# Table swish, a new stage order, ordered first loads and bf16 weight copies spread over four uses, in a two-layer three-branch encoder step

## The chip, the cores and the metric

One Trainium2 chip, with all 8 of its cores on the same program, each with its own two prompt sequences and its own rows of the sample request. Cores 0 to 3 are one die and cores 4 to 7 the other. The time is the device time in microseconds (us) of the slowest core.

In some executions the four cores of one die (or of both) show a lower granted TensorE clock and the time is some per cent longer. A run is called slow when one die is over 1% longer than the other at a lower clock, or when it is over 1.5% above the fastest run of the same kernel. Only fast runs are compared.

## The reference, cut to what matters

```python
# per layer, D = 1024; [..] cut
h = rmsnorm(x)
proj = h @ w_in            # split into the 12 column groups used below
# A: gated short convolution, 3 taps
y_a = a_b * dwconv3(a_c * a_x) * silu(a_z)
# B: Conformer convolution module, 31 taps
glu = b_in[..., :W] * sigmoid(b_in[..., W:])
y_b = silu(layernorm(dwconv31(glu) + bias, ln_b_g, ln_b_b)) * silu(b_z)
# C: chunked spatial gating, 128-token chunks
y_c = gelu(c_u) * (w_s @ layernorm(gelu(c_v)) + b_s) * silu(c_z)
m = sum_k sigmoid(g_k + gate_b_k) * (y_k @ w_branch_k)
x = x + m @ w_out
```

Each core has 9 token tiles: 5 of 512 tokens, 3 of 384 and one of 448 (384 of a prompt and the 64 sample rows). The weights arrive as float32.

## The kernel before

The kernel goes through 18 "bodies", one for each tile and layer, all on one PE stream without a break. I number them b0 to b17. The order is tile 0 and tile 1 with layer 0 (b0, b1), the same tiles with layer 1 (b2, b3), tiles 2 and 3 with layer 0 (b4, b5), with layer 1 (b6, b7), and so on. The 512-token bodies are b0 to b8 and b10. The 384-token bodies are b9 and b11 to b15, and the 448-token bodies are b16 and b17.

A body's stages are CV (projection of v), then B1 (GLU input of branch B, four steps q) interleaved with A (branch A, eight steps j), conv_b (31-tap convolution of B, eight steps, as matmuls), C, the gate Z of branch B, merge gates G with branch projections BR, and O.

All weights pass through a ring of four slots. The first use of a weight block loads it as float32 and casts to bf16 on the way, on the queue that GpSimd (POOL) issues. A bf16 copy is stored from the slot at once, on the queue that SyncE (SP) issues. Every later use reloads that copy through SP.

```python
def emit_load(n):
    l, key = plan[n]
    s = n % NSLOT                                    # NSLOT = 4
    dst_bf, w = wloc(l, key, True)
    if (l, key) not in converted:                    # first use
        converted.add((l, key))
        src, w = wloc(l, key, False)
        DMA(wring[:, s, 0:w], src, (), (("w", s),), "w%d" % s, eng="pool")
        DMA(dst_bf, wring[:, s, 0:w], (("w", s),), (("wall", l, key),), "ws%d" % s)   # store, on SP
    else:
        DMA(wring[:, s, 0:w], dst_bf, (("wall", l, key),), (("w", s),), "w%d" % s)    # reload, on SP
```

The convolution of B reads four shifted copies of the GLU output. A group of 16 DMAs per step q, all issued by SP one after another, makes them. I call one such group a replica (grep<-gluT in the profile). Times to land, below, are those of one of its 16 DMAs, of 67.6 KB.

```python
def replicate(q):
    qb = q % 2
    # [..]
    for s4 in range(4):
        for g in range(GB):                          # GB = 4
            # grep[32*s4 : 32*s4+32, :, g] <- gluT[32*g : 32*g+32, qb, :, s4 : ]
    S.dma_group("sp", fns, (("gluT", qb),), ("grep",), "rep%d" % qb)

stage_B1(0)
replicate(0)
stage_A(0)
stage_A(1)
# [..]
for q in range(1, 4):
    stage_B1(q)
    conv_b(2 * q - 2)                                # waits for replicate(q - 1)
    conv_b(2 * q - 1)
    replicate(q)
    for j in (2 * q, 2 * q + 1):
        stage_A(j)
        # [..]
conv_b(6)
conv_b(7)
```

The swish functions are made from tanh on ScalarE (ACT) and a scalar_tensor_tensor (STT) on VectorE (DVE). The layer norm of B takes a DVE reciprocal.

```python
# stage A:
ACT(z, bank_ap(bz, NT), AF.Tanh, PSR(bz), RT(tz), scale=0.5)
STT(z, z, 1.0, bank_ap(bz, NT), ALU.add, ALU.mult, ...)
# layer norm of B, after stage C 0:
ACT(var, var, AF.Sqrt, ...)
RECIP(rstd_bc[:, 0:NT], var, ...)
# per chunk j, during stage C:
TT(c, c, mean_bc, ALU.subtract, ...); STT(c, c, ln_g[j], rstd_bc, ALU.mult, ALU.mult, ...); TS(c, c, ln_b[j], ALU.add, ...)
# gate of B (stage Z), per chunk:
ACT(c, co[:, j], AF.Tanh, scale=0.5); ACT(z, bank_ap(bz, NT), AF.Tanh, scale=0.5)
STT(z, z, 1.0, bank, ...); STT(c, c, 1.0, co[:, j], ...); STT(yb[:, j], c, 0.25, z, ...)
```

Of the kernel before, what the change touches and what calls it, by code (L numbers as in the profile page):

```python
# [6 lines left out]
F32 = mybir.dt.float32  # L7
BF16 = mybir.dt.bfloat16
AF = mybir.ActivationFunctionType
ALU = mybir.AluOpType  # L10
# [21 lines left out]
class Sched:  # L32
    ENG = ("pe", "act", "dve", "pool", "sp")

    def __init__(self):
        self.streams = {e: [] for e in self.ENG}
        self.count = {e: 0 for e in self.ENG}
        self.known = {e: {} for e in self.ENG}
        self.last_w = {}
        self.readers = {}  # L40
        self.lane_n = {}
        self.bank_ptr = 0
        self.held = set()
        self.tmp_ptr = 0

# [88 lines left out]
    def tmp(self):  # L134
        i = self.tmp_ptr
        self.tmp_ptr = (i + 1) % NTMP
        return i
# [10 lines left out]
def build_program(n_seq, seq_len, with_sample=True, samp_len=64):  # L148
# [38 lines left out]
    with es:  # L187
# [129 lines left out]
        for l, T in bodies:  # L317
            plan += [(l, ("CV", 0)), (l, ("CV", 1))]
            for q in range(4):
                plan += [(l, ("B1", q)), (l, ("A", 2 * q)), (l, ("A", 2 * q + 1))]  # L320
            plan += [(l, ("CUZ", q)) for q in range(4)] + [(l, ("B2", 0)), (l, ("B2", 1))]
            for j in range(8):
                plan += [(l, ("G", j)), (l, ("BR", j))]
            plan += [(l, ("O", 0)), (l, ("O", 1))]
        converted = set()
        ring = dict(next=0, use=0)
        live = set()

        def emit_load(n):
# [3 lines left out]
            if (l, key) not in converted:  # L333
                converted.add((l, key))
                src, w = wloc(l, key, False)
                DMA(wring[:, s, 0:w], src, (), (("w", s),), "w%d" % s, eng="pool")
                DMA(dst_bf, wring[:, s, 0:w], (("w", s),), (("wall", l, key),), "ws%d" % s)
            else:
                DMA(wring[:, s, 0:w], dst_bf, (("wall", l, key),), (("w", s),), "w%d" % s)

        def ring_pump():
            while (ring["next"] < len(plan) and ring["next"] < ring["use"] + NSLOT
# [4 lines left out]
        def wget(l, key):  # L347
# [9 lines left out]
            w = 384 if key[0] in B384 else 512  # L357
            return wring[:, s, 0:8 * w].rearrange("p (k n) -> p k n", k=8), (("w", s),)
# [17 lines left out]
        def load_x(T, engs=("pool",)):  # L376
            for s, (c0, rows, xsrc, ydst) in enumerate(T["chunks"]):
                DMA(X[0:rows, T["xb"], s, :], xsrc, (), (("X", T["xb"], s),), "x%d" % s, eng=engs[s % len(engs)])

        load_x(tiles[0], ("sp", "act"))  # L380
        DMA(pc[:, :, :], prm.rearrange("p (c r) -> p c r", c=NCH), (), ("pc",), "p0", eng="act")
        ring_pump()
# [9 lines left out]
        DMA(cbq[:, :, :], cvb_in.rearrange("l p n -> p l n"), (), ("cbq",), "p1", eng="act")  # L392
        cow = co[:, :, :].rearrange("p c n -> p (c n)")
        for l in range(DEPTH):
            DMA(cow[:, l * 1024:(l + 1) * 1024], w_sq[l], (), (("co", 2 * l), ("co", 2 * l + 1)), "p%d" % (2 + l), eng="act")
            DMA(cow[:, 2048 + l * 1024:3072 + l * 1024], b_s[l].partition_broadcast(128), (),
                (("co", 4 + 2 * l), ("co", 5 + 2 * l)), "p%d" % (4 + l), eng="act")
        na, nb = DEPTH * NCH * (KA - 1), DEPTH * NCH * (KB - 1)
        DMA(tmp_t[:, 1, 0:na], ca_in, (), RT(1), "p6", eng="act")
        DMA(tmp_t[:, 2, 0:nb], cb_in, (), RT(2), "p7", eng="act")  # L400
        DMA(fg[:, :], final_g.partition_broadcast(128), (), ("fg",), "p8", eng="act")
        for l in range(DEPTH):
            r0 = l * NROW
            TS(pc[:, :, r0 + R_GB0:r0 + R_CA + KA], pc[:, :, r0 + R_GB0:r0 + R_CA + KA], 0.5, ALU.mult, ("pc",), ("pc",))
        S.tmp_ptr = 3

        def prep_caches():
            COPY(chal_a[:, :, :, :].rearrange("p a b c -> p (a b c)"), tmp_t[:, 1, 0:na], RT(1), ("chal",))
            TS(chal_b[:, :, :, :].rearrange("p a b c -> p (a b c)"), tmp_t[:, 2, 0:nb], 2.0, ALU.mult, RT(2), ("chal",))

        def prep_ws():
            for l in range(DEPTH):
                wl = cow[:, l * 1024:(l + 1) * 1024]
                rl = (("co", 2 * l), ("co", 2 * l + 1))
                S.op("pool", lambda e, wl=wl: e.affine_select(
                    out=wl.rearrange("p (g q) -> p g q", g=8), in_=wl.rearrange("p (g q) -> p g q", g=8),
                    pattern=[[0, 8], [1, 128]], compare_op=ALU.is_ge, fill=0.0, base=0, channel_multiplier=-1),
                    reads=rl, writes=rl)
                COPY(wsT[:, l].rearrange("p g q -> p (g q)"), wl, rl, (("wsT", l),))
                b2 = S.bank_n(2)  # L420

                def f(e, l=l, b2=b2):
                    ins = None
                    for h in range(2):
                        ins = e.matmul(bank_ap(b2 + h, 512), lhsT=ones[:, :],
                                       rhs=wsT[:, l, 4 * h:4 * h + 4, :].rearrange("p g q -> p (g q)"), start=True, stop=True)
                    return ins
                PE(f, (("wsT", l), "ones"), PSR(b2, b2 + 1))
                for j in range(8):
                    STT(Bc[:, l, j, :], ps[:, b2 * 512 + j * 128:b2 * 512 + (j + 1) * 128], pcol(l, j, R_LCB),  # L430
# [586 lines left out]
```

## Time and profile before

| | before |
|---|---|
| median of 3 runs | 4914.83 us (4901.43 to 5396.57) |
| profiled run, slowest core (core 1) | 4923.7 us |
| first matmul of CV; of branch B | 40 us; 71 us |
| b0, b2 (first use of a layer's weights) | 375, 364 us |
| b1, b3 to b8, b10 | 274 to 276 us |
| the six 384-token bodies | 218 to 227 us, 1337 in all |
| b16, b17 | 281, 327 us |

The durations of bodies here and below are differences between the starts of the first CV matmul of one body and of the next, read from the timeline of PE (TensorE).

From the page of the kernel before come the busy times and the chain of waits that ended last, followed back from the end and shared out by engine:

```profile
...
PE 4407.0 (90%) x25860; PEld 2134.8 (43%) x25860; DVE 2400.2 (49%) x4071; ACT 1636.5 (33%) x2684; POOL 167.2 (3%) x579
...
PE 69%; DVE 12%; DMA 6%; issue 6%; SPq 3%; ACT 3%; ACTq 1%; DVEq 0%; POOL 0%; POOLq 0%
...
```

PE is busy for 90% of the span and is 69% of the chain, so it is what bounds the kernel. The remaining 10% is what a change can win, together with PE's slow phases. What PE waited for is in the list of PE's waits of the kernel before (line waited for, then us in total, times, longest us):

```profile
...
PE ps L673 <- DMA grep<-gluT: 110.7, 13, 30.8
PE ps L484 <- DVE tmp_t L244: 109.8, 71, 3.5
PE ps L484 <- DVE yb L244: 80.9, 18, 5.5
...
```

The table of stretches splits this. Here it is for b2, b3 and for one stretch of b4 (busy us by engine with instruction counts, then granted clock, DMA share, GB/s):

```profile
...
core 1: us, PE busy (x) PEld busy (x) DVE busy (x) ACT busy (x) POOL busy (x), PEclk, DMA share, GB/s
...
689.00:1053.00 364.00, 274.72 (x1426) 120.36 (x1425) 146.91 (x219) 96.62 (x152) 23.50 (x60) 0.89 0.93 209
1053.00:1327.00 274.00, 260.40 (x1425) 117.03 (x1424) 143.14 (x216) 100.58 (x157) 8.50 (x32) 0.99 0.52 170
1448.00:1510.00 62.00, 50.47 (x245) 22.74 (x243) 54.77 (x82) 23.34 (x39) 0.00 (x0) 0.96 0.29 98
...
```

b2 does the same work as b3 and takes 90 us longer, with the DMA engines 93% busy: its weights come as float32 and are stored. That is one kind of loss. Of the 90 us, 56 are PE's waits for replicas, of which b3 has none. The last stretch is the other: from the middle of branch C to the first merge DVE is busy 54.77 of 62 us while PE is busy only 50.47. The timeline of PE of the kernel before shows what happens there (start, duration, operation, count, and in brackets the wait just before with its releaser):

```profile
...
1468.19 3.61 PE L484 MATMUL ps<-hT,wring 128*128 128x512 bf16 x16 [1.05 <-DVE tmp_t L244]
...
1473.36 3.61 PE L484 MATMUL ps<-hT,wring 128*128 128x512 bf16 x16 [1.33 <-DVE tmp_t L244]
...
1478.38 13.97 PE L484 MATMUL ps<-hT,wring 128*128 128x512 bf16 x64 [1.19 <-DVE tmp_t L244]
1495.20 6.74 PE L484 MATMUL ps<-hT,wring 128*128 128x512 bf16 x24 [2.84 <-DVE tmp_t L244]
1501.78 1.89 PE L484 MATMUL ps<-ya,wring 128*128 128x512 bf16 x8
...
1510.46 3.57 PE L484 MATMUL ps<-yb,wring 128*128 128x512 bf16 x8 [5.07 <-DVE yb L244]
...
```

Five times here PE waits for DVE, 11.5 us in all. After the last wait, of 5.07 us, eight matmuls take 3.57 us; the eight before took 1.89. After the wait of 2.84 us, 24 matmuls take 6.74 us. The granted clock (the share of full speed that TensorE was given) is 0.50 in the trace from 1495.2 to 1498 us and 0.99 in the 4 us after, and it is 0.50 again from 1510.4 to 1513.9. So a long wait costs twice: the wait, and a restart at half rate. The Trainium skill, "TensorE: Matmul & The Clock Gate", Part 1, states that an idle stretch of about 3.4 us drops the array to half rate until it has been busy that long again. This trace agrees in kind, since the 1.33 us wait above is followed by 16 matmuls at the usual pace (3.61 us), but here a wait of 2.84 us was already enough (roughly, since the profile models the ends of matmuls).

Here are the replicas in the same kernel. The first fence is from the list of DMA issues on the page (count, size, median us from issue to landing), and shows them beside the float32 loads:

```profile
...
wring<-w POOLq DMA_DIRECT2D x44, 1024.0 KB, 14.1
...
grep<-gluT SPq DMA_DIRECT2D x640, 67.6 KB, 2.4
...
```

The timeline of SP (b3 of the kernel before) has the issue of the first replica of the body, all 16 DMAs in a row:

```profile
...
1078.73 10.02 SPq L640 DMA_DIRECT2D grep<-gluT  x16
...
```

and the timeline of PE has the matmuls that have to cover it, with no wait in brackets ahead of the convolution (line 673):

```profile
...
1074.79 20.24 PE L484 MATMUL ps<-hT,wring 128*128 128x512 bf16 x93
1094.95 3.64 PE L673 MATMUL ps<-grep,dB_t 128*32 128x512 bf16 x64
...
```

Issuing takes SP 10 us. The last DMAs of the replica then have to land, and the convolution can start. Its cover is the stages A 0, A 1 and B1 1, each four projections of 8 matmuls: 96 matmuls of 216 ns, or 20.7 us. That was enough. The last replica of a body has a shorter cover in this kernel, two A stages only (64 matmuls); in the 384-token bodies, where these take 10.4 us, the convolution 6 behind them waits sometimes (8.74 us in b12, 7.73 in b15).

### The profile page before, as it was taken

The numbers are of one execution on the slowest core, as the hardware profiler recorded it, in microseconds if no ns is written. First come the engines' busy times: TensorE is split into PE (matmuls) and PEld (weight loads), VectorE is DVE, ScalarE is ACT, GpSimd is POOL, SyncE is SP. The second block draws the span as 40 slices with busy tenths as digits, with TensorE's granted clock in tenths as the row PEclk, the third lists the DMA queues.
The fourth block names the chain that finished last, engine by engine and source line by source line (L and its number), as shares of the span: only waits on it lengthen the run. The fifth ranks groups of instructions, "written<-read, shape, count | busy, mean of one in ns | idle before, by whom it ended". The sixth has DMA issues, their size and how long they took to land.

```text
span 4923.7 us, 75738 instructions; the slowest of 8 cores (4869.0 to 4923.7 us)
## 1 busy us (share of the span) xinstructions
PE 4407.0 (90%) x25860; PEld 2134.8 (43%) x25860; DVE 2400.2 (49%) x4071; ACT 1636.5 (33%) x2684; POOL 167.2 (3%) x579
## 2 busy tenths in 40 slices
PE   4789895889999999999999999989898989999898
PEld 1334342334444444443444554455455555544343
DVE  2353632536355464646354545444545454555362
ACT  2232331333332333333332333333333333332331
POOL 1000000000000000000000000000000000000000
PEclk8899997999999999999999999999999999998787
DMA  9897379985463535355464554365655647563443
GB/s 220 203 202 218 128 186 218 189 222 179 154 199 131 192 120 188 122 176 168 161 194 141 195 178 166 130 229 180 202 192 170 214 167 242 160 216 120 148 137 103
DMA packets 234727, 869.45 MB, mean 177 GB/s; under 512 B 34512, under 2 KB 108848, under 8 KB 178032
## 3 DMA queue, kind: packets, MB, share of 16 engines
q1 hardware_dynamic: 211680, 753.61, 46.1%
q0 software_dynamic: 20384, 104.61, 11.1%
q10 hardware_dynamic: 2288, 6.39, 0.5%
q8 instruction: 216, 3.54, 0.3%
q14 instruction: 159, 1.30, 0.1%
HBM read 768.97 MB, written 93.85 MB: 175 GB/s over the span
## 4 chain that ended last, share of the span: by engine, by line
PE 69%; DVE 12%; DMA 6%; issue 6%; SPq 3%; ACT 3%; ACTq 1%; DVEq 0%; POOL 0%; POOLq 0%
PE ps L484 54%; DVE tmp_t L244 6%; PE ps L834 5%; PE ps L673 5%; PE ps L534 4%; SPq L640 3%; DMA wring<-w 3%; DMA grep<-gluT 2%; DMA c<-wring 1%; DVE co L244 1%; DVE co L241 1%; DVE yc L241 1%; PE ps L658 1%; ACT cs_t L238 1%; ACTq L264 1%
## 5 line engine op out<-in xcount | busy, mean ns | idle before, releaser
L484 PE MATMUL ps<-hT,wring 128*128 128x512 bf16 (+2 forms) x13824 | 2851.8, 366 | 149.3 <-DVE tmp_t L244 109.8
L484 PEld LDWEIGHTS ps<-hT,wring 128*128 128x128 bf16 x13824 | 1364.9, 100 | 1560.3 <-issue 248.2
L244 DVE SCALAR_TENSOR_TENSOR tmp_t<-tmp_t,ps 128x512 f32<-128x512 f32 (+2 forms) x864 | 544.4, 632 | 1291.9 <-PE ps L484 646.8
L238 ACT ACTIVATE tmp_t<-ps 128x512 f32<-128x512 f32 (+2 forms) x882 | 475.0, 554 | 1096.6 <-PE ps L484 941.5
L238 ACT ACTIVATE tmp_t<-ps,pc 128x512 f32<-128x512 f32 (+2 forms) x432 | 275.0, 645 | 850.3 <-PE ps L484 835.1
L673 PE MATMUL ps<-grep,dB_t 128*32 128x512 bf16 (+2 forms) x5120 | 265.3, 356 | 119.4 <-DMA grep<-gluT 110.7
L484 PE MATMUL ps<-yb,wring 128*128 128x512 bf16 (+2 forms) x1152 | 279.2, 391 | 80.9 <-DVE yb L244 80.9
L238 ACT ACT_TABLE_LOAD x161 | 206.6, 1283 | 243.0 <-PE ps L484 83.6
L534 PE MATMUL ps<-wring,hT 128*128 128x512 bf16 (+1 forms) x1056 | 242.0, 390 | 34.1 <-DVE hT L241 34.1
L834 PE MATMUL ps<-wring,vm 128*128 128x512 bf16 (+1 forms) x1056 | 243.9, 393 | 30.9 <-DVE vm L241 15.8
L484 PE MATMUL ps<-ya,wring 128*128 128x512 bf16 (+2 forms) x1152 | 255.8, 366 | 16.7 <-DMA wring<-w 12.0
L484 PE MATMUL ps<-yc,wring 128*128 128x512 bf16 (+2 forms) x1152 | 254.8, 365 | 0.0
L673 PEld LDWEIGHTS ps<-grep,dB_t 128*32 128x32 bf16 x5120 | 125.5, 100 | 253.8 <-issue 179.7
L244 DVE SCALAR_TENSOR_TENSOR tmp_t<-tT,pc,tmp_t 128x512 f32<-128x512 bf16 (+2 forms) x320 | 209.1, 654 | 34.9 <-DVE tmp_t L244 0.2
L238 ACT ACTIVATE co<-ps,pc 128x512 f32<-128x512 f32 (+2 forms) x144 | 93.1, 646 | 380.0 <-PE ps L673 380.0
L484 PEld LDWEIGHTS ps<-yb,wring 128*128 128x128 bf16 x1152 | 118.5, 104 | 215.4 <-issue 114.1
L241 DVE TENSOR_TENSOR tT<-ps,tmp_t 128x512 bf16<-128x512 f32 (+2 forms) x160 | 94.6, 591 | 213.5 <-PE ps L484 143.2
L238 ACT ACTIVATE tmp_t<-co 128x512 f32<-128x512 f32 (+2 forms) x144 | 84.7, 589 | 284.3 <-DVE yb L244 127.9
L534 PEld LDWEIGHTS ps<-wring,hT 128*128 128x128 bf16 (+1 forms) x1056 | 105.4, 100 | 165.3 <-issue 50.0
L834 PEld LDWEIGHTS ps<-wring,vm 128*128 128x128 bf16 (+1 forms) x1056 | 105.1, 101 | 164.4 <-issue 58.4
L484 PEld LDWEIGHTS ps<-ya,wring 128*128 128x128 bf16 x1152 | 113.7, 99 | 136.2 <-issue 23.8
L238 ACT ACTIVATE cs_t<-ps,pc 128x512 bf16<-128x512 f32 (+2 forms) x288 | 169.3, 644 | 0.0
(92 smaller groups left out, 2658.6 us busy)
## 6 DMA issues: line engine op xcount, KB each, us to landing
wring<-c SPq DMA_DIRECT2D x352, 1024.0 KB, 6.0
wring<-c SPq DMA_DIRECT2D x256, 768.0 KB, 4.3
wring<-w POOLq DMA_DIRECT2D x44, 1024.0 KB, 14.1
c<-wring SPq DMA_DIRECT2D x44, 1024.0 KB, 10.7
grep<-gluT SPq DMA_DIRECT2D x640, 67.6 KB, 2.4
dB_t<-dball SPq DMA_DIRECT2D x128, 256.0 KB, 7.4
wring<-w POOLq DMA_DIRECT2D x32, 768.0 KB, 13.2
c<-wring SPq DMA_DIRECT2D x32, 768.0 KB, 13.3
```

The source lines that it names most:

```text
L238: S.op("act", lambda e: e.activation(out=out, in_=in_, func=func, **kw), reads=reads, writes=writes)
L241: S.op(eng, lambda e: e.tensor_tensor(out=out, in0=in0, in1=in1, op=op), reads=reads, writes=writes)
L244: S.op("dve", lambda e: e.scalar_tensor_tensor(out=out, in0=in0, scalar=scalar, in1=in1, op0=op0, op1=op1), reads=reads, writes=writes)
L264: S.op(eng, lambda e: e.dma_start(out=out, in_=in_), reads=reads, writes=writes, lane=lane)
L484: ins = e.matmul(bank_ap(b, NT), lhsT=w[:, kk, col0:col0 + 128], rhs=rhs[:, kk, 0:NT], start=(kk == 0), stop=(kk == 7))
L534: ins = e.matmul(ps[0:rows, (b2 + h) * 512:(b2 + h + 1) * 512], lhsT=hT[:, kk, c0:c0 + rows], rhs=wV[h][0][:, kk, :], start=(kk == 0), sto ...
L640: return e.dma_start(out=grep[32 * s4:32 * s4 + 32, :, g, 0:wb], in_=gluT[32 * g:32 * g + 32, qb, :, s4:s4 + wb])
L658: e.matmul(bank_ap(bS1, NT), lhsT=ones[:, :], rhs=cs_t[:, 2 * ci, 0:NT], start=(j == 0), stop=(j == 7))
L673: ins = e.matmul(ps[32 * g:32 * g + 32, b * 512 + c0:b * 512 + c0 + n], lhsT=dB_t[:, d, (g * MB + m) * 32:(g * MB + m + 1) * 32], rhs=grep ...
L834: ins = e.matmul(ps[0:rows, (b2 + h) * 512:(b2 + h + 1) * 512], lhsT=mT[:, kk, c0:c0 + rows], rhs=wO[h][0][:, kk, :], start=(kk == 0), sto ...
```

## The change

The intent was to take work off DVE where PE waits for it, to spread the DMA work of the first two layers over more bodies, and to bring the first matmul forward:

1. Swish by the Silu table of ACT in A and in the gate of B. The scale and bias of B's layer norm go into that Silu. The reciprocal standard deviation is Exp(-0.5 Ln(var + eps)) on ACT.
2. Another stage order. A 1 moves behind the first convolutions, convolutions 6 and 7 move ahead of stage A 7 with the layer norm right behind it, and the first merge gates move into stage Z.
3. The first loads are put in a sequence instead of all at once.
4. The bf16 copies are stored at the first, second, third or fourth use of a block, issued when the block is used. Until its copy exists, each use of the block is a float32 load: 188 of them instead of 76. In bodies 0 to 3 the small halo copies (the last tokens of one tile, which the convolutions of the next need) move from POOL to ACT.

```diff
             plan += [(l, ("CV", 0)), (l, ("CV", 1))]
-            for q in range(4):
-                plan += [(l, ("B1", q)), (l, ("A", 2 * q)), (l, ("A", 2 * q + 1))]
+            plan += [(l, ("B1", 0)), (l, ("A", 0))]
+            for q in range(1, 4):
+                plan += [(l, ("B1", q)), (l, ("A", 2 * q - 1)), (l, ("A", 2 * q))]
+            plan += [(l, ("A", 7))]
[..]
+        def store_visit(key):
+            return (2, 0, 3, 1, 2, 1)[order.index(key) % 6]
 
         def emit_load(n):
[..]
-            if (l, key) not in converted:
-                converted.add((l, key))
-                src, w = wloc(l, key, False)
-                DMA(wring[:, s, 0:w], src, (), (("w", s),), "w%d" % s, eng="pool")
-                DMA(dst_bf, wring[:, s, 0:w], (("w", s),), (("wall", l, key),), "ws%d" % s)
-            else:
+            if (l, key) in stored:
                 DMA(wring[:, s, 0:w], dst_bf, (("wall", l, key),), (("w", s),), "w%d" % s)
+                return
+            src, w = wloc(l, key, False)
+            DMA(wring[:, s, 0:w], src, (), (("w", s),), "w%d" % s, eng="pool")
+            visits[l, key] = visits.get((l, key), 0) + 1
+            if visits[l, key] > store_visit(key):
+                stored.add((l, key))
+                to_store.add(n)
[..]  in wget, at the use of a block:
+            if n in to_store:
+                DMA(wloc(l, key, True)[0], wring[:, s, 0:8 * w], (("w", s),), (("wall", l, key),), "ws%d" % s)
[..]
+            def hcopy(out, in_, reads, writes):
+                if bi < 2 * DEPTH:
+                    ACT(out, in_, AF.Copy, reads, writes)
+                else:
+                    COPY(out, in_, reads, writes, eng="pool")
[..]  stage A:
-                ACT(z, bank_ap(bz, NT), AF.Tanh, PSR(bz), RT(tz), scale=0.5)
+                ACT(z, bank_ap(bz, NT), AF.Silu, PSR(bz), RT(tz))
-                STT(z, z, 1.0, bank_ap(bz, NT), ALU.add, ALU.mult, RT(tz) + PSR(bz), RT(tz))
[..]
             stage_A(0)
-            stage_A(1)
[..]
             for q in range(1, 4):
                 stage_B1(q)
                 conv_b(2 * q - 2)
                 conv_b(2 * q - 1)
                 replicate(q)
-                for j in (2 * q, 2 * q + 1):
+                for j in (2 * q - 1, 2 * q):
                     stage_A(j)
[..]
             conv_b(6)
             conv_b(7)
[..]  layer norm of B and stage C:
-            ACT(tmp_t[:, tv, 0:NT], tmp_t[:, tv, 0:NT], AF.Sqrt, RT(tv) + ("epsc",), RT(tv), bias=epsc[:, 0:1])
-            RECIP(rstd_bc[:, 0:NT], tmp_t[:, tv, 0:NT], RT(tv), ("rstd_bc",))
+                ACT(tmp_t[:, tv, 0:NT], tmp_t[:, tv, 0:NT], AF.Ln, RT(tv) + ("epsc",), RT(tv), bias=epsc[:, 0:1])
+                ACT(rstd_bc[:, 0:NT], tmp_t[:, tv, 0:NT], AF.Exp, RT(tv), ("rstd_bc",), scale=-0.5)
[..]
-                STT(c, c, pcol(l, j, R_LBG), rstd_bc[:, 0:NT], ALU.mult, ALU.mult, ...)
-                TS(c, c, pcol(l, j, R_LBB), ALU.add, ...)
+                TT(c, c, rstd_bc[:, 0:NT], ALU.mult, ...)
[..]
+            stage_A(7, stat_b)
+            ln_b()
+            co_norm(0)
+            co_norm(1)
+            tail_out()
+            for j in range(8):
                 if j % 2 == 0:
                     wC = wget(l, ("CUZ", j // 2))
                 stage_C(j, *wC)
-                co_norm(j - 1)
+                if j < 6:
+                    co_norm(j + 2)
[..]  stage Z:
-                ACT(c, co[:, j, 0:NT], AF.Tanh, (("co", j),), RT(tc), scale=0.5)
-                ACT(z, bank_ap(bz, NT), AF.Tanh, PSR(bz), RT(tz), scale=0.5)
-                STT(z, ...); STT(c, ...); STT(yb[:, j, 0:NT], c, 0.25, z, ...)
+                ACT(c, co[:, j, 0:NT], AF.Silu, ..., scale=pcol(l, j, R_LBG), bias=pcol(l, j, R_LBB))
+                ACT(z, bank_ap(bz, NT), AF.Silu, PSR(bz), RT(tz))
+                TT(yb[:, j, 0:NT], c, z, ALU.mult, ...)
```

## The prediction

> **What bounds it now.** TensorE. The chain of waits gives PE 69%, DVE 12%, DMA 6%; PE is busy 4407 of 4924 us. The kernel is 18 bodies (9 token tiles x 2 layers); I read five kinds of loss from busy time by stretch and PE's waits (core 1):
> - Head: the first matmul of the first projection starts at 40 us, of branch B at 71.
> - Bodies 0 and 2 (first use of a layer's weights: float32 load plus bf16 store of the same slot) take 344 us (from 71) and 363, with DMA 91-93% busy; the same work in bodies 1 and 3 takes 275. The longest waits there are for the replicas of gluT (110 us in all): their queue also carries the stores, which wait for loads.
> - The eight other 512-token bodies take 275 us. In branch C, B-gate and first merge (1448 to 1510 of body 4) DVE is continuously busy and PE waits for it six times, 12 us, and twice restarts at half rate. Matmuls at their spacing (216 ns) would need about 256 us.
> - The six 384-token bodies take 219 to 227; spacing alone (162 ns) says about 193.
> - The last two (448) take 277 and 332; cores 0 and 1 run at clock 0.81 from 4480 on. Cores 2 and 3 ran at 0.76 to 0.80 from 100 to 500 us. The Trainium skill, "TensorE: Matmul & The Clock Gate" (HAM part), states a 13/16 limit for the whole die; here it held a pair of cores for some 450 us.
>
> **What the change does, per 512 body.** DVE loses 8 STT in A (0.69 us), 16 in B-gate, the 3.35 us reciprocal, 8 TS (0.49): about 24 of 142 us, nearly all inside or just before the stretch where DVE limits. Branch C plus LN falls from 4.75 to about 4.2 us per chunk against PE's 3.67; B-gate from 2.06 to 0.69 against 1.73. Moving conv 6/7 ahead starts LN one stage earlier. Costs: Silu and tanh share a table, so about one more table load per body (1.28 us here; "ScalarE: Activation LUTs", What ACT_TABLE_LOAD costs, says 1283 ns, and the trace agrees), off the path. Expected: 275 to about 261; 384 bodies 222 to about 204.
>
> Weights: 188 float32 loads instead of 76, stores spread over four uses. From queue shares a float32 load costs about 5.5 to 6 us of all engines per 1 MB block, a bf16 load or a store 3. Bodies 0 to 3 then each need about 250 us of DMA: near the limit, so I expect about 275 to 280 each, not 261. Bodies 0, 2 gain about 70 and 85; 1 and 3 nothing. Head: ordered loads save about 28 us.
>
> Sum: head 28, bodies 0 and 2 155, six 512 bodies 80, six 384 bodies 108, last two 40, about 410 to 430.
>
> **Predicted: 4490 us**, 8 in 10 within 4390 to 4640. Faster by over 2%: 0.95; within 2%: 0.04; slower: 0.01.
>
> **What would show it.** Branch B starts near 43 us; bodies 0 and 2 near 275, DMA about 0.9 there and raised in 1 and 3; steady 512 bodies 258 to 264 and PE's waits for tmp_t and yb by DVE falling from 190 us to under 60; waits for the replicas under 50; DVE busy about 2000; table loads about 180; software queue about 210 MB.
>
> **What would make it wrong.** DMA saturating in bodies 0 to 3, so that second uses get slower than 275; GpSimd's in-order queue, which holds halo copies behind float32 loads in bodies 4 to 7; DVE waiting in order for Exp at the start of C, so that its backlog still stalls PE there; and the clock limit engaging longer because PE is denser: 450 us at 0.81 costs about 85.

## The result, and the profile after

| | before | after |
|---|---|---|
| fast runs | 4891.85, 4901.43, 4914.83 us | 4728.16, 4732.03 us |
| slow runs | 5396.57 us | 5070.09, 5121.56 us |
| ratio of fast runs | 1 | 0.9648 (95%: 0.9593 to 0.9703) |
| PE's waits for replicas | 110.7 us | 223.0 us |
| DVE busy | 2400.2 us | 2024.8 us |

A ratio here and below compares the fast runs of one kernel with the other's fast runs of the same rounds; it is within 0.0002 of the ratio of their means, and not quite that of the medians. The changed kernel is faster by 3.5%. The prediction, 4490 us, was 8.6% below the time before, and its range ended at 4640. The profiled run of after is a fast one, 4726.6 us on core 6, and all its cores have a mean granted clock of 0.968 to 0.972.

From the page of the kernel after come busy times, chain, and two lines of the list of DMA issues:

```profile
...
PE 4306.4 (91%) x25860; PEld 2117.0 (45%) x25860; DVE 2024.8 (43%) x3476; ACT 1708.8 (36%) x2816; POOL 214.1 (5%) x607
...
PE 65%; DMA 10%; SPq 7%; DVE 7%; issue 6%; ACT 4%; DVEq 0%; POOL 0%; ACTq 0%; POOLq 0%
...
wring<-w POOLq DMA_DIRECT2D x112, 1024.0 KB, 11.7
...
grep<-gluT SPq DMA_DIRECT2D x640, 67.6 KB, 3.9
...
```

DMA plus SP's sequencer is now 17% of the chain, against 9% before. PE's share of the chain fell, and DVE's nearly halved. One DMA of a replica takes 3.9 us to land in the median, against 2.4. PE's waits of the kernel after:

```profile
...
PE ps L715 <- DMA grep<-gluT: 223.0, 32, 21.4
PE ps L507 <- ACT tmp_t L241: 46.5, 55, 2.6
PE ps L507 <- DVE tmp_t L247: 19.9, 43, 1.2
...
```

The two losses that the change aimed at are small or gone. The waits for tmp_t by DVE fell from 109.8 to 19.9 us, with 46.5 us now waiting for tmp_t by ACT, and the 80.9 us for yb have left the list. But the waits for the replicas doubled, from 13 to 32 of them. The merge of b5 shows the first point. In the timeline of PE of the kernel after, this is the end of stage C and the first merge:

```profile
...
1672.85 3.61 PE L507 MATMUL ps<-hT,wring 128*128 128x512 bf16 x16 [0.31 <-DVE tmp_t L247]
...
1677.20 19.15 PE L507 MATMUL ps<-hT,wring 128*128 128x512 bf16 x88 [0.52 <-ACT tmp_t L241]
1696.19 1.89 PE L507 MATMUL ps<-ya,wring 128*128 128x512 bf16 x8
...
1699.64 1.89 PE L507 MATMUL ps<-yb,wring 128*128 128x512 bf16 x8
...
```

The waits here are half a microsecond and less, and the first projection of yb runs at full pace. The second point is in the table of stretches of the kernel after, for b1, b3 and b8 (the columns are those of before):

```profile
...
337.00:627.00 290.00, 262.04 (x1425) 118.14 (x1424) 119.01 (x188) 100.26 (x172) 20.62 (x37) 0.96 0.91 188
...
933.00:1229.00 296.00, 265.18 (x1426) 119.00 (x1425) 120.52 (x184) 107.62 (x183) 20.92 (x39) 0.95 0.87 192
2351.00:2615.00 264.00, 257.76 (x1417) 117.00 (x1416) 119.40 (x183) 98.18 (x150) 8.10 (x31) 1.00 0.54 175
...
```

b8 takes 264 us against 275.5 before. b1 and b3 take 290 and 296, where before they took 274. The DMA share there is 0.91 and 0.87, where it was 0.50 and 0.52, yet the bytes moved are only 188 and 192 GB/s, against 175 in b8 with a share of 0.54. The timeline of SP of the kernel after has two of the replicas of b1:

```profile
...
361.94 10.74 SPq L682 DMA_DIRECT2D grep<-gluT  x16
...
414.05 21.13 SPq L682 DMA_DIRECT2D grep<-gluT  x16
...
```

and the timeline of PE shows the convolution (line 715) waiting for the first of them:

```profile
...
354.67 16.57 PE L507 MATMUL ps<-hT,wring 128*128 128x512 bf16 x76
382.29 5.30 PE L715 MATMUL ps<-grep,dB_t 128*32 128x512 bf16 x64 [11.05 <-DMA grep<-gluT]
...
409.20 1.91 PE L715 MATMUL ps<-grep,dB_t 128*32 128x512 bf16 x32
...
```

The replica's issue took 10.74 us from 361.94, and only at 382.29 could the convolution start. DVE's last write of gluT ended 0.14 us before the issue, so SP was not held up by other work (in b2 of before it began 17 us after that write). Between them PE now has A 0 and B1 1 alone, 64 matmuls or 13.8 us, since A 1 moved behind the convolution. The 64 convolution matmuls after the wait took 5.30 us, and twice 1.91 in the next step. The third replica took SP 21.13 us to issue. The DMA view of the kernel after says what else was on the engines from 340 to 440 us (packets, MB, share of 16 engines; then the replicas' own landing time):

```profile
...
q0 software_dynamic: 1992, 11.47, 66.8%
q1 hardware_dynamic: 4279, 7.04, 27.8%
...
grep<-gluT SPq DMA_DIRECT2D x48, 67.6 KB, 10.0
...
```

The float32 loads (q0) take 66.8% of the engines' time, and a DMA of 67.6 KB needs 10.0 us to land. The 384-token bodies have no float32 loads at all, and still PE waits in b12, in the timeline of PE of the kernel after:

```profile
...
3349.09 4.14 PE L715 MATMUL ps<-grep,dB_t 128*32 128x384 bf16 x64 [5.42 <-DMA grep<-gluT]
...
3369.63 1.49 PE L715 MATMUL ps<-grep,dB_t 128*32 128x384 bf16 x32
...
3408.53 2.75 PE L715 MATMUL ps<-grep,dB_t 128*32 128x384 bf16 x32 [5.46 <-DMA grep<-gluT]
...
```

The first wait is at convolution 0, whose cover is 64 matmuls of 162 ns (10.4 us) instead of 96 (15.6 us), while SP's issue alone takes 10.19 us there. The second is at convolution 6. Its cover is 64 matmuls too (A 5 and A 6, line 507), as many as before (A 6 and A 7). Both restarts are slow: 64 convolution matmuls take 4.14 us after the first wait, and 32 take 2.75 after the second, where 32 take 1.49 without one.

Where the time went, by stretches. The column "predicted" has the terms of the prediction, with 277.5 for each of b0 to b3 (275 for b0) after a start of branch B at 43 us. The terms add up to 4509. The text took about the upper end of its savings, 4490.

| us | before | predicted | after | after less predicted |
|---|---|---|---|---|
| end of b3 | 1328 | 1150 | 1229 | +79 |
| b4 to b7 | 1099 | 1044 | 1122 | +78 |
| b8 and b10 | 551 | 522 | 528 | +6 |
| six 384-token bodies | 1337 | 1224 | 1305 | +81 |
| b16 and b17 | 609 | 569 | 543 | -26 |
| PE's waits for replicas, in all | 111 | under 50 | 223 | |

So the gain that is missing lies in two places, b0 to b7 and the 384-token bodies. Two theories were set against each other.

- **Window.** The replicas come too late. Their path is 10 us of issue on one sequencer and then a landing that float32 loads lengthen. The new order shortened the window that covers it. Then the same bytes with a shorter issue path, or the old order, bring back much of the time.
- **Saturation.** The DMA engines cannot do more in b0 to b7 (share 0.85 to 0.91). Then only fewer float32 loads help, the issue path does not matter there, and the 384-token bodies need a cause of their own.

### The profile page after: what moved, and what is told of

It reads as the page before. It is cut to its first block, busy times and chain, and to the rows that moved or that the text cites. A ratio compares the mean times of both kernels' runs of the same rounds, so it can differ in the third digit from the quotient of the medians.

```text
span 4726.6 us, 74121 instructions; the slowest of 8 cores (4691.4 to 4726.6 us)
## 1 busy us (share of the span) xinstructions
PE 4306.4 (91%) x25860; PEld 2117.0 (45%) x25860; DVE 2024.8 (43%) x3476; ACT 1708.8 (36%) x2816; POOL 214.1 (5%) x607
## 3 DMA queue, kind: packets, MB, share of 16 engines
q0 software_dynamic: 37952, 214.84, 25.0%
## 4 chain that ended last, share of the span: by engine, by line
PE 65%; DMA 10%; SPq 7%; DVE 7%; issue 6%; ACT 4%; DVEq 0%; POOL 0%; ACTq 0%; POOLq 0%
PE ps L507 50%; SPq L682 7%; PE ps L715 6%; DMA grep<-gluT 4%; PE ps L897 4%; PE ps L557 3%; DVE tmp_t L247 3%; DMA c<-wring 2%; DMA wring<-w 1%; ACT cs_t L241 1%; ACT L241 1%; ACT gv_t L241 1%; DVE co L244 1%; DVE yc L244 1%; PE ps L700 1%
## 5 line engine op out<-in xcount | busy, mean ns | idle before, releaser
L507 PE MATMUL ps<-hT,wring 128*128 128x512 bf16 (+2 forms) x13824 | 2770.7, 359 | 93.6 <-ACT tmp_t L241 46.5
L507 PEld LDWEIGHTS ps<-hT,wring 128*128 128x128 bf16 x13824 | 1343.3, 98 | 1438.0 <-issue 131.3
L247 DVE SCALAR_TENSOR_TENSOR tmp_t<-tmp_t,ps 128x512 f32<-128x512 f32 (+2 forms) x576 | 365.4, 634 | 827.3 <-PE ps L507 577.3
L715 PE MATMUL ps<-grep,dB_t 128*32 128x512 bf16 (+2 forms) x5120 | 301.9, 390 | 239.0 <-DMA grep<-gluT 223.0
L241 ACT ACT_TABLE_LOAD x179 | 229.7, 1283 | 302.4 <-DVE tmp_t L247 95.6
L715 PEld LDWEIGHTS ps<-grep,dB_t 128*32 128x32 bf16 x5120 | 138.9, 107 | 399.0 <-issue 332.8
L897 PE MATMUL ps<-wring,vm 128*128 128x512 bf16 (+1 forms) x1056 | 232.9, 381 | 20.6 <-DVE vm L244 18.5
L507 PE MATMUL ps<-yb,wring 128*128 128x512 bf16 (+2 forms) x1152 | 248.3, 358 | 0.0
L267 POOL DMA_DIRECT2D wring<-w x188 | 103.0, 548 | 1827.4 <-PE ps L507 1015.3
L241 ACT ACTIVATE xn_t<-X 128x1024 bf16<-128x1024 f32 (+1 forms) x99 | 103.7, 1050 | 176.0 <-DVE X L247 168.6
L507 PEld LDWEIGHTS ps<-yc,wring 128*128 128x128 bf16 x1152 | 112.7, 98 | 112.0
## 6 DMA issues: line engine op xcount, KB each, us to landing
grep<-gluT SPq DMA_DIRECT2D x640, 67.6 KB, 3.9
```

Source lines behind the costliest of these rows:

```text
L241: S.op("act", lambda e: e.activation(out=out, in_=in_, func=func, **kw), reads=reads, writes=writes)
L247: S.op("dve", lambda e: e.scalar_tensor_tensor(out=out, in0=in0, scalar=scalar, in1=in1, op0=op0, op1=op1), reads=reads, writes=writes)
L267: S.op(eng, lambda e: e.dma_start(out=out, in_=in_), reads=reads, writes=writes, lane=lane)
L507: ins = e.matmul(bank_ap(b, NT), lhsT=w[:, kk, col0:col0 + 128], rhs=rhs[:, kk, 0:NT], start=(kk == 0), stop=(kk == 7))
L715: ins = e.matmul(ps[32 * g:32 * g + 32, b * 512 + c0:b * 512 + c0 + n], lhsT=dB_t[:, d, (g * MB + m) * 32:(g * MB + m + 1) * 32], rhs=grep ...
L897: ins = e.matmul(ps[0:rows, (b2 + h) * 512:(b2 + h + 1) * 512], lhsT=mT[:, kk, c0:c0 + rows], rhs=wO[h][0][:, kk, :], start=(kk == 0), sto ...
```

## The experiments

All kernels gave correct results. The kernel before was run again on each chip, and its fast runs were 4929 to 4951 us (first chip: e1, e2, e3, e4), 4908 to 4913 us (second chip: e0, e5, e6, e7). On the third chip (e8, e9, e10, e11) it was slow in all runs but one, 5058 us, which is itself disturbed, so there are no ratios from there, and only kernels of that chip are compared with one another.

The stretches of the profiled runs, as in the table above. They come from the core that the profile took, and for e0, e1, e5 and e11, whose profiled run was slow, from a core of the die left alone. Cores of one run differ: in after the end of b3 lies between 1193 and 1229 us on the eight cores, the waits for replicas between 193 and 223, the six 384-token bodies between 1298 and 1308. A difference within that spread needs the other cores too.

| us | end of b3 | b4 to b7 | b8, b10 | six 384s | b16, b17 | waits for replicas |
|---|---|---|---|---|---|---|
| before | 1328 | 1099 | 551 | 1337 | 609 | 111 |
| after | 1229 | 1122 | 528 | 1305 | 543 | 223 |
| e0 after again | 1224 | 1116 | 530 | 1304 | 545 | 221 |
| e1 copies at first use | 1275 | 1064 | 532 | 1301 | 546 | 124 |
| e2 no copies | 1216 | 1184 | 589 | 1627 | 635 | 587 |
| e3 two queues | 1174 | 1091 | 524 | 1263 | 534 | 72 |
| e4 old order | 1251 | 1128 | 521 | 1262 | 532 | 183 |
| e5 both | 1167 | 1075 | 522 | 1258 | 529 | 52 |
| e6 both, halos on ACT | 1175 | 1066 | 522 | 1255 | 530 | 66 |
| e7 swish alone | 1298 | 1054 | 527 | 1262 | 530 | 135 |
| e8 as e6, later copies | 1160 | 1093 | 522 | 1251 | 529 | 80 |
| e9 convolutions last | 1215 | 1118 | 529 | 1274 | 536 | 186 |
| e10 as e6, copies at first use | 1258 | 1044 | 522 | 1258 | 533 | 16 |
| e11 as e6, again | 1164 | 1059 | 521 | 1250 | 527 | 60 |

### e1: the copies at the first use

```diff
-            return (2, 0, 3, 1, 2, 1)[order.index(key) % 6]
+            return 0
```

> The changed kernel with every bf16 copy stored at a weight's first use (76 float32 loads instead of 188), all else as changed. Theory CONTENTION (the float32 loads of the later uses slow the replicas of gluT, which the changed order can no longer hide): bodies 1 and 3 (second uses) fall from about 294 us to 262 to 268, bodies 4 to 7 from 274-288 to 262 to 268, and PE's waits for replicas in those bodies from 25 and 10 us each to under 5; bodies 0 and 2 rise again, to 330 to 350 and 340 to 360 (from 337 and 303), since loads and stores meet there. In sum about level with the changed kernel, within 40 us. Rival WINDOW (the shorter distance between replica and conv alone costs it, whatever else moves): bodies 1 and 3 to 7 keep at least 10 us of waits each and stay above 272.

Measured: one fast run, 4743.87 us; the others were slow. In the profiled run the die left alone took 4709 to 4727 us. b1 and b3 to b7 took 265.5 to 266.6 us, against 273.8 to 295.9 in after, and b0 and b2 went up to 385 and 338. The page of e1 shows the landing of a replica back at its old time:

```profile
...
grep<-gluT SPq DMA_DIRECT2D x640, 67.6 KB, 2.4
...
```

What follows: the float32 loads of the second to fourth uses, with their stores, are what slows b1 and b3 to b7 (e2 shows that the loads do it without stores). Taking them away gives back 24 us in b1, 29 in b3 and 58 in b4 to b7 (after less e1), and costs 67 in b0 and 33 in b2. In the changed kernel, spreading the copies gains and loses about the same.

### e2: no copies at all

```diff
-            return (2, 0, 3, 1, 2, 1)[order.index(key) % 6]
+            return 99
```

> The changed kernel with no bf16 copies at all: all loads are float32 for the whole run, no stores. Doubles the suspected cost. CONTENTION: the 512-token bodies from body 8 on rise from 264 to about 285 to 300 us and the 384-token ones from 217 to 240 or more, with 20 to 30 us of waits for replicas in each; total about 5000 to 5150 us. WINDOW: bodies 8 and later do not change (264 and 217), total about 4730.

Measured: 5253.38 us, the fast run, more than expected. PE waited 586.5 us for replicas, in all bodies: b8 took 302 us and the 384-token bodies 267 to 274. There are no stores here, so stores on SP's queue cannot be the cause. The page of e2 has the landing:

```profile
...
grep<-gluT SPq DMA_DIRECT2D x640, 67.6 KB, 7.9
...
```

All three of these kernels and before issue the replicas from SP alone. The median landing times of the 67.6 KB DMAs line up with the number of float32 loads: 2.4 us with 76 of them (e1, and before), 3.9 with 188 (after), 7.9 with 684 (e2). The contention half of the window theory is shown.

### e3: the replicas issued from two queues

```diff
                 for s4 in range(4):
+                    if s4 == 2:
+                        S.dma_group("sp", fns, (("gluT", qb),), ("grep",), "rep%d" % qb)
+                        fns = []
                     for g in range(GB):
[..]
-                S.dma_group("sp", fns, (("gluT", qb),), ("grep",), "rep%d" % qb)
+                S.dma_group("act", fns, (("gluT", qb),), ("grep1",), "arep%d" % qb)
[..]  in conv_b:
-                PE(f, ("grep", ("dB", d)), PSR(b))
+                PE(f, ("grep", "grep1", ("dB", d)), PSR(b))
```

> The changed kernel with the 16 issues of each replica (0.6 us each, 10 us in a row on one queue) split over two queues, 8 each; bytes and order stay. WINDOW (replica needs 10 us of issue plus 2 to 4 us of landing; only 13.8 us of matmuls, 10.4 with 384 tokens, now cover it): PE's waits for replicas fall from 223 us to under 100, 384-token bodies from 217 to about 207, total about 4600 to 4640. CONTENTION (landing, not issuing, is slow): bodies 0 to 3 gain only the 5 us of each exposed replica, waits stay above 120, total 4660 to 4700.

Measured: fast runs 4582.93 and 4589.28 us, a little below what the window theory expected. The bytes and the loads are those of after. A single replica DMA of SP's half takes longer to land (6.1 us in the median against 3.9), but the group is complete earlier, as its issue takes SP 5.7 us in the median instead of 10.9. Whether the second queue helps in another way too, this run cannot tell. PE's waits of e3:

```profile
...
PE ps L718 <- DMA grep<-gluT: 71.5, 13, 17.4
...
```

What follows: saturation as the whole cause falls, since the same DMA work fits in some 140 us less. The 384-token bodies lost 42 us (1305 to 1263) and b0 to b3 55 us. b1 and b3 at 287 and 280 us remain above the 266 of e1, so part of the excess there stays even with the shorter issue.

### e4: the order of before

```diff
-            plan += [(l, ("B1", 0)), (l, ("A", 0))]
-            for q in range(1, 4):
-                plan += [(l, ("B1", q)), (l, ("A", 2 * q - 1)), (l, ("A", 2 * q))]
-            plan += [(l, ("A", 7))]
+            for q in range(4):
+                plan += [(l, ("B1", q)), (l, ("A", 2 * q)), (l, ("A", 2 * q + 1))]
[..]
             stage_A(0)
+            stage_A(1)
[..]  convolutions 6 and 7 behind A 7 again, layer norm behind stage C 0, as before
```

> The changed kernel with the order of before: A 0 and A 1 between the first replica and conv 0, conv 6 and 7 behind A 7, LN behind the first chunk of C; Silu, Ln/Exp, loads and copies as changed. WINDOW: the wait for the first replica of a body vanishes in bodies 4 and later (384-token bodies lose about 5 of their 11 us of replica waits), and is 7 us shorter in bodies 0 to 3, so waits fall from 223 to about 120; in exchange C starts with a backlog of DVE and 2 to 5 us per body come back; total about 4680 to 4730. CONTENTION alone: waits stay at 200 or more, total 4730 to 4800.

Measured: 4688.80, 4695.56, 4695.59 and 4743.10 us, all fast, ratio 0.9525 to the kernel before (0.9413 to 0.9637). The waits at convolution 0 in the 384-token bodies vanish: those bodies take 1262 us, 43 less than in after. b8 is 260.3 us with the layer norm later, so moving it ahead was worth nothing there. The first four bodies do not gain; the end of b3 is 22 us later than in after (1230 to 1252 us on the eight cores, against 1193 to 1229), and in all the waits for replicas are 183 us, not the 120 of the window theory. The merge gates stay in stage Z in this run, so it is not the whole old order. Convolution 6 still waits in some 384-token bodies, 1.5 to 10.8 us each, as it does in before.

b4 and b6 got slower than b5 and b7 (293 and 289 us) with a wait of another kind. The timeline of POOL of e4 shows why: the float32 load of a ring slot waits for the store out of that slot, and the halo copy of stage A stands behind it in POOL's order:

```profile
...
1297.98 0.53 POOL L267 DMA_DIRECT2D wring<-w  x1 [20.08 <-DMA c<-wring]
1298.50 0.20 POOL L262 COPY tT<-hal_a 128x2 bf16<-128x2 bf16 x1
...
```

The timeline of PE of the same moment waits for tT, which that halo copy completes:

```profile
...
1299.64 5.66 PE L713 MATMUL ps<-grep,dB_t 128*32 128x512 bf16 x64 [7.51 <-DVE tT L244]
...
```

This is the in-order queue of GpSimd that the prediction named as a risk. It is also in after, smaller (7.9 us in all).

### e7: the swish and the layer norm alone, on the kernel before

```diff
 (kernel before)
-                ACT(z, bank_ap(bz, NT), AF.Tanh, PSR(bz), RT(tz), scale=0.5)
+                ACT(z, bank_ap(bz, NT), AF.Silu, PSR(bz), RT(tz))
-                STT(z, z, 1.0, bank_ap(bz, NT), ALU.add, ALU.mult, RT(tz) + PSR(bz), RT(tz))
[..]  Ln and Exp for Sqrt and RECIP; Silu in stage Z, with the layer norm's scale and bias in it
```

> The kernel before with the table swish in A and B and the rstd by Ln and Exp alone (no change of order, loads, copies). If the wait for DVE in C, B-gate and first merge was the loss of steady bodies as predicted: 512-token bodies from 275 to 260 to 262, 384-token ones from 222 to 204 to 208, bodies 0 and 2 keep 345 and 350 or more; total 4900 less 250 to 280, so 4630 to 4680, below the whole change. If the gain in steady bodies needs the new order too: 265 or more, total above 4720.

Measured: 4673.26, 4677.64, 4683.66 and 4700.79 us fast, with a fifth run slow, ratio 0.9538 (0.9486 to 0.9590). This part of the change alone gains more than the whole, whose ratio was 0.9648; on this same chip the whole (e0, next) took 4760.65 us in its one fast run. b1, b3, b5, b6 and b10 took 260 to 262 us, and the 384-token bodies 1262, 210 each. The prediction had 261 and 204. b0 and b2 stay at 375 and 360. PE's waits of e7:

```profile
...
PE ps L672 <- DMA grep<-gluT: 135.0, 18, 32.5
...
```

### e0: the changed kernel again

No edit; a repeat, beside e5, e6 and e7 on one chip.

> The changed kernel, unaltered, on the chip of the next three runs, as their yardstick: undisturbed dies at about 4700 us, fast runs 4730 to 4760.

Measured: one fast run, 4760.65 us, with die 1 a little disturbed; in the other runs one die was slow, and the other took 4708 to 4748 us. The stretches repeat those of after within 6 us each, and the waits for replicas are 221 us. The pattern of the changed kernel is not a chance of one run.

### e5: old order and two queues together

The edits of e3 and e4.

> The changed kernel with both mends: stage order of before (first replica covered by A 0, A 1 and B1 1) and the replicas' issues split over two queues. If the replicas are the cause of the missing gain: waits for them fall below 50 us (223 in the changed kernel, 72 with two queues, 183 with the old order), bodies 8 and 10 take 260, 384-token bodies 204 to 207, bodies 1 to 3 275 to 282, total 4520 to 4550. If the old order's gain in bodies 8 and later was already in the two queues' gain: total stays at 4560 to 4590.

Measured: no fast run in six, so no time and no ratio can be given; the lowest was 4624.97 us. In the dies left alone it took 4523 to 4561 us. On such a core the waits for replicas are 52 us, b1 to b3 276 to 281, b5 and b7 262. b4 and b6 are still at 281 and 269, with PE waiting for tT. The 384-token bodies take 210, not the 204 to 207 expected. With two queues the order matters little: e3, in the new order, has 1263 us for these bodies where e5 has 1258, and 524 for b8 and b10 where e5 has 522.

### e6: e5 with the halo copies on ACT in the first eight bodies

```diff
 (e5)
-                if bi < 2 * DEPTH:
+                if bi < 4 * DEPTH:
                     ACT(out, in_, AF.Copy, reads, writes)
```

> As the run before, and the small halo copies stay on ScalarE for the first eight bodies instead of four. Theory: in bodies 4 to 7 GpSimd's in-order queue holds halo copies behind float32 loads that wait for the store of the same slot (17 to 20 us each in the trace of the old order), which delays gluT and so the convs: bodies 4 and 6 fall from about 285 and 275 to 265 to 270, total 20 to 30 us less than the run before. Rival (those bodies are slow from load on the DMA engines): no change.

Measured: 4543.84, 4545.23, 4548.63 and 4549.63 us, four of four fast, ratio 0.9258 (0.9231 to 0.9285). This version beats both kernels. The waits for tT are gone, and b4 and b6 fell by 9 and 4 us against e5; b4 now waits 6.2 us for a replica. On all its cores e6 takes 1057 to 1066 us for b4 to b7, and the four undisturbed cores of e5 1073 to 1086. As a gain in time over e5 that cannot be stated, since e5 had no fast run; the undisturbed dies, 4523 to 4561 of e5 and 4509 to 4549 of e6, allow about 10 us, less than the 20 to 30 expected. PE's waits of e6:

```profile
...
PE ps L716 <- DMA grep<-gluT: 66.5, 8, 22.7
...
```

### e9: only convolutions 6 and 7 and the layer norm moved back

```diff
+            stage_A(7)
             conv_b(6)
             conv_b(7)
[..]
-            stage_A(7, stat_b)
-            ln_b()
[..]  layer norm behind stage C 0, as before; A 1 stays behind the first convolutions
```

> The changed kernel with conv 6, conv 7 and LN back behind A 7, but A 1 still behind the first convs: the short distance for the first replica of a body stays (A 0 and B1 1 alone), the last one is longer (A 5, A 6, A 7). Splits the cost of the new order. FIRST REPLICA: 384-token bodies keep the wait of about 5 us at conv 0 and lose the one at conv 6; they take 208 to 214, bodies 8 and 10 take 262 to 264; bodies 1 to 3 stay at 288 to 300; total 4690 to 4720. LAST REPLICA: nearly all the waits of bodies 8 and later vanish, total under 4680.

Measured: 4656.02, 4672.76 and 4675.37 us fast, the size that the last-replica theory expected, though the stalls are not as it said. The 384-token bodies take 1274 us, between after (1305) and e4 (1262). The timeline of PE says which stall is which: in e9 convolution 0 still waits in every one of them (3.7 to 6.1 us, with 64 matmuls of cover), and convolution 6, whose cover is now three A stages, waits in two only (3.03 and 2.80 us). In e4 and in before it is the other way round, apart from waits under 0.7 us. b8 and b10 are 264.7 and 264.5 us, as in after (264.1, 264.4), and not 260.3 as in e4; their only wait for replicas is that of convolution 0.

What follows for the bodies without float32 loads: it is A 1's new place that costs against before, through the first window. Putting convolutions 6 and 7 ahead of A 7 was neutral for the last window, since it is two A stages in both orders, and it gained nothing in b8 and b10. Behind a full A 7, as in e9, the last window would be better than in either kernel; with A 1 at its old place there is no such stage left. The numbers are from three chips, but where the replicas are not waited for b8 is 260.3 to 262 us on all of them (e3 to e6, e8, e10, e11).

### e10 and e11: what the spread copies are worth once the replicas are mended

e10 is e6 with copies at the first use (`return 0` as in e1). e11 is e6 again, on the same chip.

> The best version so far, but every bf16 copy stored at the first use (76 float32 loads instead of 188). Asks what the copies over four uses are worth once the replicas and halo copies no longer stand in the way. From the sums of bodies 0 to 7 (2222 us in the best version; 385 and 338 for bodies 0 and 2 with first-use stores, 262 for the rest): total about 4600 to 4630, so 50 to 80 us slower than 4547. If the copies over four uses are worth nothing: within 20 us of 4547.

> The best version so far once more, unaltered, as the yardstick of these four runs: 4540 to 4560 in the fast state, and a ratio of 0.92 to 0.93 to the kernel before.

Measured: e10 4606.36 and 4616.78 us fast, e11 4526.35 and 4538.71 us fast. The spread copies are worth 79 us (means 4611.6 and 4532.5), where in the changed kernel they were worth nothing clear. In e10 b1 and b3 to b7 take 261 to 262 us and the waits for replicas are 16 us in all. So without float32 loads in later uses these bodies do reach what the prediction had for them.

### e8: the sixth group of copies at the fourth use

```diff
 (e6)
-            return (2, 0, 3, 1, 2, 1)[order.index(key) % 6]
+            return (2, 0, 3, 1, 2, 3)[order.index(key) % 6]
```

> The best version so far (old stage order, two queues for the replicas, halo copies on ScalarE through body 7) with one of six weights stored at its fourth use instead of its second, so that bodies 1 and 3 store less and bodies 4 to 7 load a little more float32. If bodies 1 to 3 are at the limit of the DMA engines: bodies 1 and 3 fall by 3 to 10 us, bodies 4 to 7 rise by 0 to 4 each, total 4530 to 4548. If not: no change beyond 10 us.

Measured: 4546.63, 4547.50 and 4556.48 us fast, against 4526.35 and 4538.71 of e11 on the same chip. On the two profiled cores b0 to b3 gained 4 us and b4 to b7 lost 34; but that core of e8 is an outlier, and between the medians of e8's eight cores and e11's four undisturbed ones b0 to b3 differ by 1 us and b4 to b7 lost 12. It saves nothing, and the mean of the fast runs is 18 us longer.

## Why the prediction was right or wrong

**Right: what DVE costs in the steady bodies.** The prediction read from the profile that DVE limits from branch C to the first merge, and put the gain at 14 us for a 512-token body. e7 does that part alone and has five 512-token bodies of 260 to 262 us instead of 274 to 276. DVE was predicted busy for about 2000 us and was for 2024.8. Table loads: about 180 predicted, 179 counted, at 1283 ns each, and off the path. Silu and tanh do share a table here: in b8 of after there is no table load from 2403 to 2473 us, where the Silu of A and the tanh of B1 alternate.

**Right: the head and the DMA volume.** Branch B's first matmul started at 47.6 us, 43 predicted, 71 before. The software queue moved 214.84 MB, about 210 predicted. Its time grew from 11.1% of 4923.7 us to 25.0% of 4726.6, which is 635 us for 112 more float32 loads, 5.7 us each, as estimated (5.5 to 6). The shares of DMA in b0 to b3, 0.85 to 0.91, are what was expected.

**Wrong: "waits for replicas under 50", and the sizes built on it.** They are 223.0 us. The prediction counted whether the DMA engines can move the bytes in time, and not how long a small transfer with a consumer waiting for it takes among them. Three terms of the sum came out wrong, mostly by that one omission:

- "Bodies 0 to 3 [...] about 275 to 280 each". They were 289 (from branch B's first matmul, as predicted for b0; 318 from the first CV matmul), 290.7, 305.6 and 295.9, 79 us too long at the end of b3. The waits for replicas in these four are 112.5 us.
- b4 to b7 counted as steady bodies at "about 261". They still have float32 loads: of the 38 blocks of a layer, 31 are loaded as float32 in the second use, 19 in the third and 6 in the fourth. They took 288.0, 273.8, 280.7 and 279.4 us, 78 too long. e1, without those loads, has 1064 us for the four instead of 1122, and e10 has 1044, the predicted sum.
- "384 bodies 222 to about 204". They took 213 to 223, 81 us too long. 55 us of that are waits for replicas, and slow restarts add to it. No float32 loads run there. The old order brings back 43 us (e4, 1262), and with two queues as well the six take 1255 (e6), with 2 us of waits for replicas left. The other 31 us, 5 a body, are not the replicas': there 204 was too low. In e6 PE waits 65 us in these six bodies, 33 of them for tmp_t by ACT (20 in before), to which the change gave work; whether that is the 31 us was not tested.

In all the fast runs of after lie 240 us above the 4490 predicted. e6, with the replicas and the halo copies mended, brings back 183 of them (4547, on another chip), so late replicas are most of the miss and not all of it.

**Wrong in sign: the order.** "Moving conv 6/7 ahead starts LN one stage earlier" was counted as a help, and the move of A 1, which came with it, not costed at all. The ratios are 0.9538 for the swish alone (e7), 0.9525 with the ordered loads, the spread copies and the merge gates in Z but the rest of the old order (e4), which is nothing more, and 0.9648 with the new order (after). The last step is a loss of 60 us by the ratios (which come from different chips and have intervals that overlap), 24 us between the means of the fast runs and 33 us between the spans of the profiled cores. By stretches e4 is 61 us faster than after from b8 on and 28 us slower before. The clear part is in the 384-token bodies: 1261 to 1268 us on the eight cores of e4, 1298 to 1308 on those of after. There the first replica lost A 1 from its cover, and the earlier layer norm gained nothing.

**Right as a risk, small in size.** POOL's in-order queue, and second uses getting slower than 275, were both named. The clock limit did not engage longer: cores 0 and 1 of before ran at 0.79 from 4480 to 4900 us, and in the fast run of after b16 and b17 took 543 us, 26 less than predicted. No run explains when this limit comes, so that term is luck as much as reading.

**Saturation as a rival** explains less than it seems to, since e3 fits the same transfers into 140 us less. It is not nothing: in e6 b2 and b3 are still 284 and 295 us with a DMA share of 0.91 and 0.88 and waits for replicas of 13 and 23 us. But b1 of e6 takes 270.5 us with a share of 0.95, so a share of 0.9 alone does not set the time.

**Open.** A replica lands late beside float32 loads, but no run separates the ways in which this can happen (turns between queues on an engine, the rate of the engine, or something that holds SP's issue back, as the 21 us issue suggests). The Trainium skill, "DMA: Bandwidth & Descriptors", Queues, rings and completion order, states that an engine takes turns between its queues packet by packet; that would fit, and no run here shows it. The end of b3 comes 22 us later in the old order (e4) than in the new one (after). The waits for replicas in b0 to b3, 137 us against 112.5, account for it; why they are longer although the first window is longer was not followed up.

## What to carry to other kernels

A DMA budget in busy time says whether bytes fit; it does not say when a small transfer on the critical path lands. Before adding background loads or moving stages, list every transfer that a consumer waits for, with its issue time, its landing time under the new load, and the work that covers both. Test the parts of a bundle separately: here one part alone (0.9538) beat the bundle (0.9648), and the bundle with its waiting transfers mended and the old stage order (e6, 0.9258) beat both.

## What the Trainium skill lacked or had wrong

- "DMA: Bandwidth & Descriptors", Issuing engines are not separate DMA queues, states that issuing from several engines saves only sequencer time, "which is usually small relative to the DMA itself". Here it was not small: the 16 DMAs of a replica, of 67.6 KB each, took SP 10.0 us or more to issue (0.63 us each) and 2.4 us each to land in before, and issuing half of them on ACT took the kernel from 4730 to 4586 us (means of the fast runs, on different chips) and the waits from 223.0 to 71.5 us.
- No page gives the landing time of a small transfer beside casting loads from GpSimd: 2.4 us with 76 of them in the kernel, 3.9 with 188, 7.9 with 684, and 10.0 us in a stretch where they took 66.8% of the engines' time.
- "TensorE: Matmul & The Clock Gate", Part 1, states that dense matmuls on three cores take the whole die to 13/16 and hold it there while the load lasts. In the fast runs of after and of e6 all eight cores ran matmuls, PE 91% busy in after, at a mean clock of 0.968 to 0.987 for 4.5 to 4.7 ms. In slow runs one die fell to a mean of about 0.81 while the other, on the same program, had 0.98 (e3: 0.812 to 0.816 and 0.983 to 0.985). The same part gives about 3.4 us of idling for the drop to half rate; here 2.84 us was enough once (24 matmuls in 6.74 instead of 5.34 us, the clock at 0.50 for the first 2.8 us).
- "ScalarE: Activation LUTs", Table sets, does not list which set holds Silu. Here Silu in place of tanh in two stages, with Ln and Exp in place of Sqrt, raised the table loads from 161 to 179, one per body, at 1283 ns each, which is what the page states for the load itself (What ACT_TABLE_LOAD costs).
